# Weight chunks of four blocks instead of two, and the residual in DRAM during the FFNs, in a decoder layer

## The chip, the cores and the metric

The kernel runs on one core of one Trainium2 chip. The metric is the device time of one execution in microseconds (us). Five engines with instruction streams of their own work side by side and wait for each other by semaphores: TensorE (PE: matmuls, with the weight loads listed apart as PEld), VectorE (DVE), ScalarE (ACT), GpSimd (POOL) and SyncE (SP), which issues most of the DMAs.

## The reference

One decoder layer on 256 tokens of width 2048, in float32: a SwiGLU FFN of width 5504 as a half step, a mixer of two gated linear attentions, and a second SwiGLU half step. Each sub-layer has an RMSNorm before it and one after it, ahead of the residual add.

```python
def swiglu(x, w_gate, w_up, w_down):
    return (jax.nn.silu(x @ w_gate) * (x @ w_up)) @ w_down

    f1 = swiglu(rms_norm(h, ffn1_pre_norm[l]), ffn1_w_gate[l], ffn1_w_up[l], ffn1_w_down[l])
    h = h + 0.5 * rms_norm(f1, ffn1_post_norm[l])
    m = hybrid_token_mixer(rms_norm(h, mix_pre_norm[l]), l, w_in[l], ...)
    h = h + rms_norm(m, mix_post_norm[l])
    f2 = swiglu(rms_norm(h, ffn2_pre_norm[l]), ffn2_w_gate[l], ffn2_w_up[l], ffn2_w_down[l])
    h = h + 0.5 * rms_norm(f2, ffn2_post_norm[l])
```

The mixer projects its input with w_in into eleven pieces (queries, keys, values, gates), runs two chunked linear attentions, weights both with sigmoid gates, adds them and projects with w_out. Nearly all of the work is in the products with the weight matrices, which are read from HBM once.

## The kernel before

**A product.** Each float32 operand is split into a rounded part (hi, made by ACT) and a rest (lo, made by DVE: value minus hi), both in the fast float32r format. One product of a 128x128 piece of the activations with a 128x512 block of weights is three matmuls, hi*hi, lo*hi, hi*lo (`mm3`, lines 157 to 159). The 256 tokens are two tiles, t = 0 and 1. PE's results collect in PSUM tiles.

**Weights.** `wload` and `wchunk` (lines 129 to 148) bring a chunk of two 128x512 blocks by one DMA of SP into a raw buffer; `split_into` (line 150) makes hi (ACT, line 151) and lo (DVE, line 153), each in one instruction of 1024 columns. The pool `ring` has five buffers each of raw, hi and lo, 1024 columns wide (RING = 5, RW = 1024). A raw buffer is free again when DVE has made lo from it, a hi and a lo buffer when PE has used them.

**Units and sevens.** `gemm_pair` (line 329) computes two output blocks i = 0, 1 for both token tiles. Its depth of 2048 is 8 units of two weight rows of blocks, so a unit has four weight blocks and eight products. Some units are computed as a "seven", with seven products instead of eight, from sums and differences of weight blocks (`Blocks.seven`, line 265; the activations' sums are made once by `operand_sums`). A seven loads its four blocks with four DMAs of one block into two raw buffers, ra and rb. DVE makes three sums more (lines 279, 281, 283), into a row tile `wsum` and back into rb; ACT makes the hi parts (lines 278, 280, 282, 284); DVE the lo parts (the three adds under `issue_after` and behind it, line 243 in the profile, since `add` is a helper). Row tiles come from the pool `rows`: three buffers of 3x512 columns, all under one tag. A seven takes three of them, for wsum and for its hi and lo part (wsumh, wsuml). `Blocks.share` (line 304), which ends the sevens of a block, takes two, and `operand_sums` and `sums_of` take some too.

The lists SUMS (units 2, 4, 6) and FOUR (2, 4, 5, 6) say which units are sevens; the FFN's eleven blocks of `w_gate` and `w_up` have none in the first block of FFN 1, then FOUR and SUMS in turn. The mixer's pairs use SUMS, and FOUR where its sums are there. The list `steps` (line 346) sets the order. With SUMS the sevens stand in their natural places; with FOUR and with `late=True` (five pairs of the mixer) they stand with half a plain unit, one chunk, between them:

```python
        if late:
            at = range(6, 6 + 2 * len(sevens), 2)
        elif len(sevens) > len(SUMS):
            at = range(3, 3 + 2 * len(sevens), 2)
```

`down_proj` (line 587) goes through w_down in two halves of 1024 columns, with six sevens in each half (DSUMS and DMORE), and holds the last DTAIL = 7 rows of the second half back, split in buffers that are free by then, so that token tile 0 can be finished first. `out_proj` (line 534) does the same for w_out with TAIL = 4. Both load the next stage's first chunks ahead (`following`, AHEAD = 3 in out_proj). `gemm_block` (line 161) is the plain form; with `held` it computes tile 0 over the whole depth first and keeps the chunks for tile 1.

**Side work.** Transposes, norms and the attentions are Python generators in `Side`; `pump` advances them by a step between the products.

**The residual** h is eight SBUF tiles of 128x512 (line 110). During the mixer it lies in DRAM (`away`, line 112), and its SBUF tiles hold gates.

**The order of work.** The framework that builds the kernel lays out each engine's instructions in order of priority, that of the program where nothing stands against it, and gives tiles of one tag their buffers as these come free. On the chip each engine runs its list in order.

Of the kernel before, what the change touches and what calls it, by code (L numbers as in the profile page):

```python
# [7 lines left out]
F32 = mybir.dt.float32  # L8
# [7 lines left out]
P = 128  # L16
# [11 lines left out]
RW = 2 * CB  # L28
STEPS = ((3, 2, 2, 2), (6, 1, 1, 1))
RING = 5  # L30
AHEAD = 3
# [55 lines left out]
def kernel(ctx: ExitStack, tc: tile.TileContext, a: dict, out: bass.AP):  # L87
# [22 lines left out]
    h = [[hpool.tile([P, CB], F32, name=f"h{t}_{n}") for n in range(4)] for t in range(NT)]  # L110

    away = [[dram.tile([P, CB], F32, name=f"away{t}_{n}") for n in range(4)] for t in range(NT)]
# [10 lines left out]

    def ring_alloc(w):
        hi, lo = [ring.tile([P, RW], F32R, tag=s, name=nm(s))[:, :2 * w]
                  .rearrange("p (i c) -> p i c", i=2) for s in ("whi", "wlo")]
        return [(hi, lo)]

    def wload(src: bass.AP, w: int, apart=False):
        raw = ring.tile([P, RW], F32, tag="raw", name=nm("raw"))[:, :2 * w].rearrange(  # L130
            "p (i c) -> p i c", i=2)
        for i in range(2) if apart else [slice(0, 2)]:
            nc.sync.dma_start(raw[:, i, :], src[:, i, :])
        return raw, apart

    def wchunk(src: bass.AP, w: int, alloc=ring_alloc, raw=None):


        raw, apart = raw or wload(src, w)
        parts = alloc(w)  # L140
        if len(parts) == 1:
            hi, lo = parts[0]
            for i in range(2) if apart else [slice(0, 2)]:
                split_into(hi[:, i, :], lo[:, i, :], raw[:, i, :])
            return [(hi[:, i, :], lo[:, i, :]) for i in range(2)]
        for i, (hi, lo) in enumerate(parts):
            split_into(hi, lo, raw[:, i, :])
        return parts
# [12 lines left out]
    def gemm_block(w_dram, c0, w, lhs, nkt=KT, held=None, raws=(), ready=()):  # L161
# [4 lines left out]
        raws, ready = list(raws), list(ready)  # L166
        nb = -(-w // CB)
        step = 2 // nb
        pss = [[ps_tile(f"mm{t}") for _ in range(nb)] for t in range(NT)]

        def chunk(k0, alloc):
            if ready:
                return ready.pop(0)
            raw = raws.pop(0) if raws else None
            src = w_dram[k0 * P:(k0 + step) * P, c0:c0 + w]
            return wchunk(src.rearrange("(k p) c -> p k c", p=P) if nb == 1 else
                          src.rearrange("p (n c) -> p n c", n=nb), w // nb, alloc, raw)

        def mm(t, k0, parts):
            for i, part in enumerate(parts):  # L180
                kt = k0 + i % step
                mm3(pss[t][i // step][:, :w // nb], lhs(t, kt), part, kt == 0, kt == nkt - 1)

        if held is None:
            for k0 in range(0, nkt, step):
# [3 lines left out]
                side.pump()  # L189
        else:  # L190
            kept = []
            for i, k0 in enumerate(range(0, nkt, 2)):
                kept.append((k0, chunk(k0, ring_alloc if i < RING else held)))
                mm(0, *kept[-1])
                side.pump()
            for k in kept:
                mm(1, *k)
                side.pump()
# [46 lines left out]
    class Blocks:  # L245
# [19 lines left out]
        def seven(self, u, end):  # L265
            w, k0 = self.w, 2 * u
            ra, rb = [ring.tile([P, RW], F32, tag="raw", name=nm("raw"))[:, :2 * w]
                      .rearrange("p (i c) -> p i c", i=2) for _ in range(2)]
            wsum, hi, lo = [row_tile(n, d)[:, :, :w] for n, d in
                            (("wsum", F32), ("wsumh", F32R), ("wsuml", F32R))]  # L270

            nc.sync.dma_start(ra[:, 0, :], self.block(0, k0))
            nc.sync.dma_start(ra[:, 1, :], self.block(1, k0 + 1))
            nc.sync.dma_start(rb[:, 0, :], self.block(1, k0))
            nc.sync.dma_start(rb[:, 1, :], self.block(0, k0 + 1))

            (ahi, alo), (bhi, blo) = ring_alloc(w) + ring_alloc(w)
# [1082 lines left out]
```

## Time and profile before

| | |
|---|---|
| median of 3 runs | 2084.71 us (2083.17 to 2084.87) |
| profiled execution, first to last instruction | 2083.3 us |
| PE, PEld busy | 2069.5 us (99%), 1722.0 us (83%) |
| DVE, ACT busy | 1855.3 us (89%), 1240.8 us (60%) |
| moved by DMA | 412.24 MB, 198 GB/s in the mean |
| granted TensorE clock, mean | 0.998 |

The profiled execution's time is known as its span. In lists of groups a row has the line, the engine, the operation, out<-in by the program's names, the count, then busy time and mean duration in ns, then the idle time before and what ended it. In a timeline a row has the start and the duration in us, then engine, line and operation; brackets give idle time before it. In a list of waits a row has who waited for whom, the us in total, the times and the longest. FFN 1 runs to about 680 us, the mixer to about 1394, FFN 2 to the end.

### The profile page before, as it was taken

Reading aid. Unit: us, or ns where it says so; the run is one execution under the profiler, and the core shown is the slowest. Engines: PE = TensorE matmul, PEld = TensorE weight load, DVE = VectorE, ACT = ScalarE, POOL = GpSimd, SP = SyncE. Lnnn points to the kernel's source line nnn. Section 1 sums busy time; section 2 is a strip of 40 time slices with the busy share of each in tenths; the row PEclk is TensorE's granted clock in tenths of the full one; section 3 lists DMA queues with packets and bytes.
Section 4 is the critical chain, followed back from the end, with each engine's and each line's share of the span. In section 5 each row is a group of like instructions: output and inputs, shape, how many; then the busy total and the mean of one; then the engine's idle time right before and its main releaser. Section 6 shows DMA issues by size and latency. Waiting matters only on the chain.

```text
span 2083.3 us, 29324 instructions
## 1 busy us (share of the span) xinstructions
PE 2069.5 (99%) x10509; PEld 1722.0 (83%) x10509; DVE 1855.3 (89%) x2187; ACT 1240.8 (60%) x1670; POOL 40.7 (2%) x87
## 2 busy tenths in 40 slices
PE   9999999999999999999999999999999999999998
PEld 7888888898888888878888888888888888898886
DVE  7898999989899779989999897578999989999896
ACT  6555656566666575576655554465555655666663
POOL 1000000000000100000000000010000000000000
PEclk9999999999999999999999999999999999999999
DMA  8666656667767466555566566755665656576663
GB/s 267 184 209 201 213 187 197 210 185 223 216 191 235 148 201 210 159 172 188 178 195 195 178 220 216 221 182 171 222 197 188 207 187 225 164 238 202 202 206 128
DMA packets 200666, 412.24 MB, mean 198 GB/s; under 512 B 18036, under 2 KB 26423, under 8 KB 200520
## 3 DMA queue, kind: packets, MB, share of 16 engines
q1 hardware_dynamic: 194896, 401.80, 60.9%
q10 hardware_dynamic: 5624, 8.57, 1.4%
q8 instruction: 82, 1.34, 0.3%
q14 instruction: 64, 0.52, 0.1%
HBM read 406.11 MB, written 4.19 MB: 197 GB/s over the span
## 4 chain that ended last, share of the span: by engine, by line
PE 96%; ACT 2%; DVE 1%; issue 1%; DMA 0%; POOL 0%; SPq 0%; DVEq 0%; POOLq 0%; ACTq 0%
PE c L157 22%; PE c L159 21%; PE c L158 21%; PE p L159 5%; PE p L157 5%; PE p L158 5%; PE mm L157 3%; PE mm L159 3%; PE mm L158 3%; PE ps L397 2%; PE acc L157 1%; PE acc L158 1%; PE acc L159 1%; PE ps L905 0%; DVE h L510 0%
## 5 line engine op out<-in xcount | busy, mean ns | idle before, releaser
L151 ACT ACTIVATE whi<-raw 128x1024 fp32r<-128x1024 f32 (+3 forms) x498 | 511.0, 1033 | 284.8 <-PE c L158 116.8
L153 DVE TENSOR_TENSOR wlo<-raw,whi 128x1024 fp32r<-128x1024 f32 (+3 forms) x498 | 587.7, 1190 | 85.5 <-ACT whi L151 84.2
L157 PE MATMUL c<-whi,xhi 128*128 128x512 f32 (+1 forms) x1270 | 495.8, 391 | 0.1
L159 PE MATMUL c<-wlo,xhi 128*128 128x512 f32 (+1 forms) x1270 | 490.9, 387 | 0.0
L158 PE MATMUL c<-whi,xlo 128*128 128x512 f32 (+1 forms) x1270 | 490.6, 386 | 0.0
L243 DVE TENSOR_TENSOR wlo<-raw,whi 128x1024 fp32r<-128x1024 f32 (+1 forms) x252 | 294.5, 1202 | 12.2 <-ACT whi L278 6.1
L159 PEld LDWEIGHTS c<-wlo,xhi 128*128 128x128 f32 x1270 | 238.5, 188 | 47.5 <-DVE wlo L153 0.3
L157 PEld LDWEIGHTS c<-whi,xhi 128*128 128x128 f32 x1270 | 238.6, 188 | 46.3 <-ACT xhi L469 0.5
L158 PEld LDWEIGHTS c<-whi,xlo 128*128 128x128 f32 x1270 | 238.7, 188 | 45.0
L282 ACT ACTIVATE whi<-raw 128x1024 fp32r<-128x1024 f32 (+1 forms) x126 | 131.8, 1046 | 203.9 <-DVE raw L243 80.9
L243 DVE TENSOR_TENSOR wsuml<-wsum,wsumh 128x1536 fp32r<-128x1536 f32 (+1 forms) x126 | 218.1, 1731 | 36.8 <-ACT wsumh L284 36.5
L157 PE MATMUL c<-whi,hkhi 128*128 128x512 f32 x558 | 217.0, 389 | 0.0
L159 PE MATMUL c<-wlo,hkhi 128*128 128x512 f32 x558 | 216.8, 388 | 0.0
L158 PE MATMUL c<-whi,hklo 128*128 128x512 f32 x558 | 216.7, 388 | 0.0
L280 ACT ACTIVATE wsumh<-wsum 128x1024 fp32r<-128x1024 f32 (+1 forms) x126 | 131.6, 1045 | 107.4 <-DVE wsum L243 70.5
L278 ACT ACTIVATE whi<-raw 128x1024 fp32r<-128x1024 f32 (+1 forms) x126 | 131.6, 1044 | 103.0 <-PE c L158 87.7
L243 DVE TENSOR_TENSOR wsum<-raw,raw 128x1024 f32<-128x1024 f32 (+1 forms) x126 | 151.8, 1205 | 21.6 <-DMA raw<-in_ffn_w_down_dram 18.1
L159 PEld LDWEIGHTS c<-wlo,hkhi 128*128 128x128 f32 x558 | 104.7, 188 | 21.6
L158 PEld LDWEIGHTS c<-whi,hklo 128*128 128x128 f32 x558 | 104.7, 188 | 21.4
L157 PEld LDWEIGHTS c<-whi,hkhi 128*128 128x128 f32 x558 | 104.7, 188 | 21.1
L243 DVE TENSOR_TENSOR c<-c,psum 128x512 f32<-128x512 f32 (+1 forms) x135 | 86.5, 683 | 11.8 <-PE c L159 11.4
L243 DVE TENSOR_TENSOR wsum<-raw 128x512 f32<-128x512 f32 (+1 forms) x126 | 86.0, 683 | 3.5
(347 smaller groups left out, 3119.4 us busy)
## 6 DMA issues: line engine op xcount, KB each, us to landing
raw<-in_ffn_w_down_dram SPq DMA_DIRECT2D x124, 512.0 KB, 4.5
raw<-in_w_in_dram SPq DMA_DIRECT2D x104, 512.0 KB, 4.5
raw<-in_ffn_w_up_dram SPq DMA_DIRECT2D x97, 512.0 KB, 4.6
raw<-in_ffn_w_gate_dram SPq DMA_DIRECT2D x96, 512.0 KB, 4.7
raw<-in_ffn_w_gate_dram SPq DMA_DIRECT2D x128, 256.0 KB, 3.7
raw<-in_w_in_dram SPq DMA_DIRECT2D x128, 256.0 KB, 3.5
raw<-in_ffn_w_up_dram SPq DMA_DIRECT2D x126, 256.0 KB, 3.8
raw<-in_ffn_w_down_dram SPq DMA_DIRECT2D x96, 256.0 KB, 4.2
```

What stands on the lines that cost most here:

```text
L151: last[0] = nc.scalar.activation(hi, src, AF.Copy)
L153: nc.vector.tensor_tensor(lo, src, hi.bitcast(F32), op=ALU.subtract)
L157: nc.tensor.matmul(ps, lhsT=xhi, rhs=whi, start=start, stop=False)
L158: nc.tensor.matmul(ps, lhsT=xlo, rhs=whi, start=False, stop=False)
L159: nc.tensor.matmul(ps, lhsT=xhi, rhs=wlo, start=False, stop=stop)
L243: return nc.vector.tensor_tensor(o, x, y, op=op)
L278: nc.scalar.activation(ahi, ra, AF.Copy)
L280: nc.scalar.activation(hi[:, 0:2, :], wsum[:, 0:2, :], AF.Copy)
L282: nc.scalar.activation(bhi, rb, AF.Copy)
L397: end = nc.tensor.transpose(dst_ps[:, i * P:(i + 1) * P], src[:, i * P:(i + 1) * P], ident)
```

## The change

A chunk becomes four blocks, so that one ACT and one DVE instruction make hi and lo of 2048 columns.

- RW is 2048, RING 3 (hi and lo), and raw buffers are counted apart: RAWS = 2. `raw_tile` takes a raw buffer; while `roomy` is set, two of four turns take a buffer of the tag "hold" instead, the place of the residual.
- The residual is one tile per token tile, under the tag "hold". FFN 2 stores it to DRAM (`away2`) after its first block of w_gate; FFN 1 doesn't store it, since it is the input x. `residual()` in the second half of `down_proj`, after unit 6, clears `roomy` and loads it back. `roomy` is set after the first block of each FFN.
- A plain unit of `gemm_pair` is one chunk: two DMAs of two blocks each into one raw buffer, one split. In `gemm_block` a chunk is four rows of weights, in `out_proj` one row by 2048 columns, in `down_proj` two rows by 1024.
- A seven takes one raw buffer and three row tiles. Two of its four blocks are loaded into the row tile `own`. Four columns of blocks, two loaded and two sums, stand in raw; two loaded blocks and one sum stand in own. The products from raw come first, the three from own last.
- The order of sevens in steps of whole units: FOUR at (1, 3, 5, 6), late at (3, 4, 5), SUMS at their own places.
- AHEAD is 2, the `hn` tiles are gone (the product is formed in the silu tile), and the tail of `down_proj` is taken in chunks of one, two and four rows. The last FFN piece of 384 columns moves to the activations' place.

The matmuls are the same ones. Core of the diff:

```diff
-RW = 2 * CB
+RW = 4 * CB
-RING = 5
-AHEAD = 3
+RING = 3
+RAWS = 2
+AHEAD = 2
...
+    def raw_tile(w):
+        turn[0] += 1
+        if roomy[0] and turn[0] % (RAWS + NT) >= RAWS:
+            raw = hpool.tile([P, RW], F32, tag="hold", name=nm("raw"), bufs=NT)
+        else:
+            raw = ring.tile([P, RW], F32, tag="raw", name=nm("raw"), bufs=RAWS)
+        return raw[:, :4 * w].rearrange("p (i c) -> p i c", i=4)
...
         def seven(self, u, end):
-            ra, rb = [ring.tile([P, RW], F32, tag="raw", name=nm("raw"))[:, :2 * w]
-                      .rearrange("p (i c) -> p i c", i=2) for _ in range(2)]
-            wsum, hi, lo = [row_tile(n, d)[:, :, :w] for n, d in
-                            (("wsum", F32), ("wsumh", F32R), ("wsuml", F32R))]
...
+            raw = raw_tile(w)
+            own, ohi, olo = [row_tile(n, d)[:, :, :w] for n, d in
+                             (("wsum", F32), ("wsumh", F32R), ("wsuml", F32R))]
+            load(raw, 1, self.block(0, k0))
+            load(raw, 0, self.block(1, k0))
+            load(own, 0, self.block(1, k0 + 1))
+            load(own, 1, self.block(0, k0 + 1))
+            hi, lo = ring_alloc(w)[0]
+            add(raw[:, 2, :], raw[:, 1, :], raw[:, 0, :])
+            nc.scalar.activation(hi[:, 1:3, :], raw[:, 1:3, :], AF.Copy)
+            add(raw[:, 0:4:3, :], raw[:, 0:3:2, :], own[:, 0:1, :].broadcast_to([P, 2, w]))
+            nc.scalar.activation(hi[:, 0:4:3, :], raw[:, 0:4:3, :], AF.Copy)
+            summed = add(own[:, 2, :], raw[:, 3, :], own[:, 1, :])
+            last[0] = nc.scalar.activation(ohi, own, AF.Copy)
             with tc.issue_after(summed.ins):
+                add(lo, raw, hi.bitcast(F32), ALU.subtract)
+            add(olo, own, ohi.bitcast(F32), ALU.subtract)
+            shared, single = [[(x[:, i, :], y[:, i, :]) for i in range(n)]
+                              for x, y, n in ((hi, lo, 4), (ohi, olo, 3))]
...
+            self.product("p1", self.lhs(0, k0), shared[1], end)
+            self.product("p6", self.part("s2", u), shared[3], end)
+            self.product("p5", self.part("d", u), shared[2], end)
+            self.product("p7", self.part("s3", u), shared[0], end)
             side.pump()
+            self.product((0, 1), self.part("s4", u), single[0])
+            self.product((0, 0), self.lhs(0, k0 + 1), single[1])
+            self.product((1, 0), self.lhs(1, k0 + 1), single[2])
             side.pump()
...
+    def load_unit(ws, u, w):
+        raw = raw_tile(w)
+        for i, (w_dram, c0) in enumerate(ws):
+            load(raw, slice(2 * i, 2 * i + 2), rows_of(w_dram, 2 * u, 2, c0, w))
+        return raw
...
-        steps = [(u, i) for u in range(nu) if u not in sevens for i in range(2)]
+        steps = [u for u in range(nu) if u not in sevens]
         if late:
-            at = range(6, 6 + 2 * len(sevens), 2)
+            at = range(3, 3 + len(sevens))
         elif len(sevens) > len(SUMS):
-            at = range(3, 3 + 2 * len(sevens), 2)
+            at = (1, 3, 5, 6)
         else:
-            at = [2 * u - j for j, u in enumerate(sevens)]
+            at = sevens
...
+            def residual():
+                roomy[0] = False
+                new_h()
+                for t in range(NT):
+                    nc.sync.dma_start(hrow[t], a["x"][t * P:(t + 1) * P, :].rearrange(
+                        "p (n c) -> p n c", c=CB) if begin else away2[t])
...
             return down_proj(a[pre + "_w_down"], FKT, lhs, sums_of, post, pre_next,
-                             [held_x] + [ring_alloc] * 2 + [held] * 4, then)
+                             [(1, held_x), (2, ring_alloc), (4, held)], residual, then)
```

More of the change, by code (lines that the diff above doesn't have):

```diff
@@ L624, in down_proj @@
             units = sorted(DSUMS + DMORE[hf])
-            kt = 0
-            while kt < n:
-                u = kt // 2
-                if kt % 2 == 0 and u + 1 in units and u + 1 not in parts:
+            for kt in range(0, n, 2):
+                u, m = kt // 2, min(2, n - kt)
+                if u + 1 in units and u + 1 not in parts:
                     parts[u + 1] = sums_of(u + 1)
@@ L691, in held @@
             def held(w):
[L692 to L694 removed]
+                return [[fpool.tile([P, 2, w], F32R, tag="hT", name=nm("held"), bufs=FKT // 4)
+                         for _ in range(2)] for _ in range(2)]
             xl = lhs_of(x)
```

337 lines of the change are left out of this document (175 added, 162 removed).

## The prediction

> **What bounds the kernel now.** I read the page's totals first, then PE's own waits, then the chain that ended last.
>
> ```profile
> span 2083.3 us, 29324 instructions
> PE 2069.5 (99%) x10509; PEld 1722.0 (83%) x10509; DVE 1855.3 (89%) x2187; ACT 1240.8 (60%) x1670; POOL 40.7 (2%) x87
> PE 96%; ACT 2%; DVE 1%; issue 1%; DMA 0%; POOL 0%; SPq 0%; DVEq 0%; POOLq 0%; ACTq 0%
> ```
> ```profile
> PE p L157 <- ACT hqT L839: 2.5, 1, 2.5
> PE ps L1300 <- POOL idle L1295: 1.3, 1, 1.3
> ```
>
> The reader is to see that TensorE (PE) carries 96% of the chain, and that in 2083 us it waited for another engine hardly ever: the one wait of note is 2.5 us. A modelled end can hide small gaps, so the pitch of the matmuls is read next: three of them, one product (hi*hi, lo*hi, hi*lo), start 0.68 us before the next three (302.91 to 303.59). A plain unit of four weight blocks is eight products, 5.44 us; a seven is seven products, 4.76 us. So PE bounds the kernel, and its work is the same in both kernels: the lists of sevens and the products in each are unchanged.
>
> ```profile
> 302.91 0.39 PE L157 MATMUL c<-whi,xhi 128*128 128x512 f32 x1
> 303.59 0.39 PE L157 MATMUL c<-whi,xhi 128*128 128x512 f32 x1
> ```
>
> That leaves two questions: which waits of PE can go, and which can come. VectorE (DVE) is the engine that could make them. Stage by stage (columns: PE, PEld, DVE, ACT, POOL busy with counts, clock, DMA share, GB/s; two blocks of FFN 1, then one of the mixer):
>
> ```profile
> 264.00:306.00 42.00, 42.00 (x191) 34.85 (x190) 40.27 (x40) 24.36 (x29) 0.00 (x0) 1.00 0.58 186
> 306.00:348.00 42.00, 42.00 (x192) 34.84 (x190) 38.24 (x40) 24.25 (x28) 0.00 (x0) 1.00 0.68 214
> 968.00:1010.00 42.00, 42.00 (x434) 34.03 (x433) 41.46 (x70) 29.02 (x48) 0.99 (x2) 1.00 0.53 165
> ```
>
> DVE is busy 40.27 and 38.24 of 42 us in the FFN, 41.46 in the mixer, and PE is never idle beside it. DVE is nearly the second bound; PE is still the first.
>
> **The merged instructions.** Their prices, by form:
>
> ```profile
> L153 DVE TENSOR_TENSOR wlo<-raw,whi 128x1024 fp32r<-128x1024 f32 x462 | 558.4, 1218 | 75.3 <-ACT whi L151 74.0
> L151 ACT ACTIVATE whi<-raw 128x1024 fp32r<-128x1024 f32 x462 | 484.9, 1056 | 267.2 <-PE c L158 110.3 <-issue 36.6 <-PE mm L158 34.5
> L243 DVE TENSOR_TENSOR wsuml<-wsum,wsumh 128x1536 fp32r<-128x1536 f32 x119 | 208.6, 1753 | 36.4 <-ACT wsumh L284 36.1
> L243 DVE TENSOR_TENSOR wsum<-raw 128x512 f32<-128x512 f32 x119 | 82.1, 690 | 3.3
> L284 ACT ACTIVATE wsumh<-wsum 128x512 fp32r<-128x512 f32 x119 | 73.5, 618 | 8.0 <-DVE wsum L243 8.0
> ```
>
> DVE takes 0.69, 1.22 and 1.75 us for 512, 1024 and 1536 columns, 0.53 a step; 2048 is then 2.28 us (estimate). ACT takes 0.62 and 1.06 us; 1536 is 1.49 and 2048 1.93 us (estimates). Merging 462 splits into 231 saves DVE 231 x (2 x 1.218 - 2.28) = 36 us. In a seven DVE had 512+512+1024+1024+1024+1536, that is 6.8 us, and gets 512+512+1024+2048+1536, 6.6 us: 119 times, 19 us more. ACT saves 231 x 0.18 + 119 x 0.19 = 64 us. All of it lies beside PE: the path gains nothing, except perhaps at the single 2.5 us wait for ACT. After that wait the matmuls start 0.43 us apart instead of 0.23 for about nine of them:
>
> ```profile
> 763.01 0.39 PE L157 MATMUL c<-whi,xhi 128*128 128x512 f32 x1
> 765.86 0.50 PE L157 MATMUL p<-whi,xs 128*128 128x512 f32 x1 [2.46 <-ACT hqT L839]
> 766.70 0.63 PE L157 MATMUL p<-wsumh,xs 128*128 128x512 f32 x1
> 767.13 0.63 PE L158 MATMUL p<-wsumh,xs 128*128 128x512 f32 x1
> ```
>
> So the wait costs 2.6 us and the slow stretch 8 x 0.2 = 1.6 us: 4.2 us is all that the middle of the kernel can give back. I take 0, since the wait is for a transpose copy (L839), not for a split.
>
> **The new load into a seven's own tile.** Here lies the price. Before, a seven loads its four blocks into two of five raw buffers, and DVE writes the sums into a row tile. After, two blocks land by DMA directly in a row tile (own). Row tiles have three buffers under one tag, and a seven takes all three: own, and the rounded and rest halves of it, ohi and olo. In the next seven, own's load can start only when olo of this one has been made, for olo is the last reader of own; and ohi waits until PE is done with this seven's last products, as the row halves already do:
>
> ```profile
> ACT wsumh L280 <- PE c L158: 36.2, 39, 7.4
> ```
>
> A load costs, over the five "late" blocks of the mixer,
>
> ```profile
> DMA to landing us min/median/max: 2.6/3.8/5.3
> ```
>
> I take 2.6, as SP has been blocked and the queue is empty. Now the late blocks: their order was plain halves between the sevens, and becomes seven, seven, seven. Count from T, where PE ends the first: ohi of the second 1.49, olo 1.75, own of the third lands 2.6 later, DVE adds (1024) 1.22, ACT rounds 1.06, DVE's rest (2048) 2.28: T + 10.4. PE meanwhile has the second seven and two matmuls of the third, 4.76 + 0.45 = 5.2 us. PE stands for 5.2 us, whatever lead DVE had: 5 blocks, 26 us.
>
> The second seven can be late as well. Its own load starts when the first's olo ends, and its rest is ready 2.6 + 1.22 + 1.06 + 2.28 = 7.2 us after that, where PE wants it 2.04 us (three products) after wanting olo. A lead under 5.1 us is then a wait. The leads before, in a late block and in a FOUR block of the FFN:
>
> ```profile
> 907.96 1.75 DVE L243 TENSOR_TENSOR wsuml<-wsum,wsumh 128x1536 fp32r<-128x1536 f32 x1
> 909.76 0.50 PE L159 MATMUL p<-wsuml,xs 128*128 128x512 f32 x1
> ```
> ```profile
> 289.12 1.76 DVE L243 TENSOR_TENSOR wsuml<-wsum,wsumh 128x1536 fp32r<-128x1536 f32 x1 [0.50 <-ACT wsumh L284]
> 292.48 0.39 PE L159 MATMUL p<-wsuml,hkhi 128*128 128x512 f32 x1
> ```
>
> DVE ends at 909.71 and PE takes it at 909.76: no lead. In the FFN it ends at 290.88 and is taken at 292.48: 1.6 us. With no lead the late block pays 5.1 us for the second and, since olo then follows its rest by 1.75 where PE has 2.72, 5.1 - 1.0 = 4.1 for the third: 9.2 in all, against 5.2 with full lead. I take 2 us a block over the floor: 10 us. For the clock, half of the 1.6 us seen above, five times: 4 us. The Trainium skill, TensorE: Matmul & The Clock Gate, Part 1, has the clock halved after an idle window of about 3.4 us and for one such window; here 2.46 us was enough. By that page five waits over 3.4 us would cost an estimated 5 x 1.7 = 8.5 us, and the sum would be 4.5 us higher.
>
> FOUR blocks (five in each FFN, two in the mixer by the code's alternation) get one pair of adjacent sevens each. The wait is 5.1 less the lead: 0 if DVE is 5 us ahead, which the order of ohi and olo just allows, 3.5 us with the 1.6 us of today. I take the middle, 1.7: 12 times, 20 us. SUMS blocks keep plain units between the sevens (10.2 us a pair against a chain of 2.6 + 1.22 + 1.06 + 2.28 + 1.75 = 8.9): nothing.
>
> Against all of these: PE's order is fixed when the kernel is built, and may be fixed so that the two products of the next plain unit that no seven touches go first, 1.36 us each of 17 times, 23 us. The records show the order as written; between 0 and 23 I take 12 off.
>
> **The smaller edits.** Raw buffers fall from five of two blocks to two of four, and four while the residual is out. The landings:
>
> ```profile
> raw<-in_w_in_dram SPq DMA_DIRECT2D x104, 512.0 KB, 4.5
> raw<-in_w_in_dram SPq DMA_DIRECT2D x128, 256.0 KB, 3.5
> ```
>
> By these 1 MB lands in about 6.5 us (estimate); with the split, 1.93 + 2.28, one slot turns in 10.7, two give a unit each 5.4 us, against PE's 5.44 in plain stretches. That is just enough in the mixer; the bounds are 0 and 0.5 us a unit (below). In FFN 1's first block PE has to start on two units instead of two and a half: 0 to 4, I take 2. At the end of each down projection seven weight rows pass the two slots while PE wants them within two units: 0 to 4 each, I take 4 for both. The residual is a matter of bytes and of SP's queue:
>
> ```profile
> DMA packets 200666, 412.24 MB, mean 198 GB/s; under 512 B 18036, under 2 KB 26423, under 8 KB 200520
> ```
>
> It adds 6 MB to 412 (one reload in FFN 1, a store and a reload in FFN 2) at a DMA share of 0.53 to 0.68; its reload sits in SP's queue between weight loads, and waits there until both of its buffers are split: 0 to 6.5 each, I take 3 for both. Below nothing none of these can go, for PE shows no wait there now. The pumps move, but their number per block stays.
>
> Sum: 26 + 10 + 4 + 20 - 12 + 2 + 4 + 3 = 57 us. The profiled execution spans 2083.3, the median of the runs is 2084.7, 1.4 more (launch edges and run to run). 2083.3 + 57 + 1.4 = 2142 us.
>
> **The rivals.** (1) PE hides it: the order leaves every seven a lead of over 5 us, and lighter ACT work removes the wait at 763 us. It decides if PE shows no wait for a rest at all. Gain up to 4.2: 2080.5. For it: DVE has 55 us less to do. Against: in the late block DVE had no lead at all. (2) It is hidden, and nothing else moves: 2084.7. (3) Only the coarser pieces count: a product waits for a rest of 2.28 where 1.22 was enough, so leads under 1.06 us turn into waits, three sevens in the late block shown, 3.2 us, 2088. The Trainium skill, Perfetto Trace Analysis, Optimizing Scalar/DVE Operations, says that where Scalar/Vector aren't saturated but make bubbles elsewhere, instructions should be broken up; a DVE at 89% is near that case. (4) Two raw slots bind the mixer: its ten blocks of two weights, eight units each, lose 0.5 us a unit to queueing behind attention on DVE (41.46 of 42 us), 40 us, without any wait for own: 2125. For: 5.4 against 5.44. Against: PE may run three chunks behind the splits.
>
> **How the numbers follow.** Forecast 0.62, (1) 0.12, (2) 0.07, (3) 0.07, (4) 0.12. A difference under 0.2%, 4 us, is about what measuring can't tell from none. Faster 0.12; same 0.07 + 0.07 = 0.14; slower 0.62 + 0.12 = 0.74. The low end takes in (2) and (3) and ends at (1): 2080. At the high end late blocks cost 9.2 + 1.6 each (54), FOUR blocks 2.5 (30), the small edits 18: 102, 2187. The forecast's own range is 2104 (the floor of 26 less 5 x 1.36, and nothing else) to 2187.
>
> **What would show it.** PE waits for "wlo" or for the own tile's rest in the third seven of each late block, about 5 us, with clock digits below 9 from 840 to 1100 us; SP's queue waiting for the DVE line that makes olo; rests of 2048 columns near 2.28 us; DVE's busy time down by about 55. The forecast is wrong if PE's busy share stays at 99% and PE's waits hold no such line, or if they name DMA into raw instead.

## The result, and the profile after

The changed kernel takes 2297.8 us (median of 4 runs, 2296.6 to 2303.3) against 2084.8: ratio 1.103, 95% interval 1.102 to 1.104, 213 us slower. The forecast was 2142: the direction is right, but the loss is nearly four times the 57 us of the sum, and the time lies far above the range of 2104 to 2187.

The page's totals of the changed kernel, and the shares of its chain:

```profile
span 2295.1 us, 27656 instructions
...
PE 2154.4 (94%) x10509; PEld 1743.9 (76%) x10509; DVE 1830.9 (80%) x1812; ACT 1196.4 (52%) x1295; POOL 51.0 (2%) x87
...
PE 6%; DVE 3%; DMA 2%; issue 1%; ACT 1%; POOL 0%; SPq 0%; DVEq 0%; POOLq 0%; ACTq 0%
```

The span grew by 211.8 us. PE's idle time grew by 126.9 of these (140.7 against 13.8), and its busy time by 84.9 for the same 10509 matmuls: they start further apart. No other engine filled up: DVE fell from 89% to 80% busy. The chain's shares add up to 13%, so it was lost on the way and can't be read here. PE's waits can (in total, times, longest):

```profile
PE p L170 <- ACT whi L296: 60.7, 28, 4.4
PE c L170 <- ACT whi L164: 20.9, 10, 4.2
PE p L172 <- DVE wlo L259: 14.3, 27, 1.5
```

L296 rounds a seven's second pair of weights, which DVE makes with a block that lands in the own tile. That wait is new. DVE's, and what SP's queue waited for:

```profile
DVE raw L259 <- DMA wsum<-in_ffn_w_up_dram: 92.0, 44, 4.6
DVE raw L259 <- DMA wsum<-in_w_in_dram: 40.6, 14, 5.5
DVE raw L259 <- DMA wsum<-in_ffn_w_down_dram: 16.7, 9, 3.4
```
```profile
SPq L150 <- DVE wlo L259: 755.0, 111, 13.6
...
SPq L150 <- DVE wsuml L259: 64.6, 76, 3.6
```

So DVE waits 149 us for the own tile's load. SP's first row is the wait for a free raw tile (e10 comes back to it); in the second, 76 times, the own tile's load waits for the last reader of the seven before (wsuml, olo in the code). One FOUR block of FFN 1 shows how. SP's issues, then DVE, then PE (start, duration, what; in brackets the idle time before):

```profile
314.31 0.37 SPq L150 DMA_DIRECT2D raw<-in_ffn_w_gate_dram  x1
314.73 0.47 SPq L150 DMA_DIRECT2D raw<-in_ffn_w_up_dram  x1
315.98 0.34 SPq L150 DMA_DIRECT2D wsum<-in_ffn_w_up_dram  x1
```
```profile
314.20 1.75 DVE L259 TENSOR_TENSOR wsuml<-wsum,wsumh 128x1536 fp32r<-128x1536 f32 x1
320.27 1.23 DVE L259 TENSOR_TENSOR raw<-raw,wsum 128x1024 f32<-128x1024 f32 x1 [4.32 <-DMA wsum<-in_ffn_w_up_dram]
...
322.62 2.29 DVE L259 TENSOR_TENSOR wlo<-raw,whi 128x2048 fp32r<-128x2048 f32 x1 [0.40 <-ACT whi L296]
324.83 1.75 DVE L259 TENSOR_TENSOR wsuml<-wsum,wsumh 128x1536 fp32r<-128x1536 f32 x1
```
```profile
318.18 0.39 PE L171 MATMUL c<-whi,xlo 128*128 128x512 f32 x1
322.64 0.80 PE L170 MATMUL p<-whi,hkhi 128*128 128x512 f32 x1 [4.07 <-ACT whi L296]
...
323.66 0.63 PE L170 MATMUL p<-whi,hkhi 128*128 128x512 f32 x1
324.09 0.63 PE L171 MATMUL p<-whi,hklo 128*128 128x512 f32 x1
```

DVE ends olo at 315.95, SP issues the next own load 0.03 us later, behind the 1 MB of the next plain unit that it issued 1.2 to 1.7 us before; DVE has the load at 320.27. From the end of one olo to the end of the next (324.83 + 1.75 = 326.58) one turn takes **10.63 us**. PE needs 4.76 us between two adjacent sevens and 10.2 where a plain unit lies between them. So DVE gains no lead in the block, and at the adjacent pair PE stands for 4.07 us and then starts a matmul each 0.43 us instead of 0.23. What the whole block looks like, with the next one (columns as in the prediction's windows):

```profile
282.00:334.00 52.00, 46.93 (x196) 36.94 (x195) 41.59 (x35) 26.18 (x23) 0.00 (x0) 0.93 0.52 177
334.00:376.00 42.00, 40.46 (x181) 32.68 (x180) 34.38 (x27) 19.96 (x17) 0.00 (x0) 1.00 0.55 181
```

The first row holds the FOUR block shown: 52 us for 196 matmuls, where 42 us held 191 in the kernel before.

Where it all went is seen from the sevens, 126 in each kernel, counted in order of time. The mark of a seven is the start of the weight load of its last matmul (c<-wsuml). The table takes the marks of each kernel, less those of the kernel before, and gives what each stretch adds; e1, e12 and e16 are experiments below. The last column is what the new order of sevens and plain units would do to the marks by itself, with PE always busy; it is the same for the four kernels, and has to be taken off each of them.

| stretch (sevens) | changed | e1 | e12 | e16 | order alone |
|---|---|---|---|---|---|
| up to the first (0) | 1.4 | 2.9 | 1.6 | 0.3 | 0 |
| FFN 1, pairs of up and gate (0 to 34) | 48.8 | 1.2 | 0.8 | 0.5 | 0 |
| FFN 1, down (34 to 46) | 10.2 | 4.3 | 2.7 | 0.1 | 0 |
| into the mixer (46 to 52) | 8.0 | 8.3 | 13.9 | -0.7 | 0 |
| mixer, late blocks (52 to 67) | 41.0 | 13.7 | 9.9 | 4.2 | -5.4 |
| behind them (67 to 68) | 14.6 | 15.1 | 11.7 | 2.7 | 2.7 |
| rest of the mixer's pairs (68 to 78) | 9.7 | 1.4 | -0.8 | 3.1 | 2.7 |
| mixer to FFN 2 (78 to 79) | 17.8 | 17.9 | 20.1 | -1.9 | -2.7 |
| FFN 2, pairs (79 to 110) | 48.1 | 4.0 | 3.1 | 2.9 | 2.7 |
| FFN 2, end and down (110 to 125) | 10.5 | 2.7 | 2.4 | 0.2 | 0 |
| sum | 210.1 | 71.5 | 65.4 | 11.4 | 0 |

The last column comes from the code: half a plain unit is 2.72 us of products, the third seven of a late block now stands two halves earlier, and the first of a FOUR block one half. It is the work, not the waits, that lies elsewhere; in e12, where PE is full in the FOUR blocks, mark 17 comes 2.7 us earlier against the kernel before than marks 16 and 18 do. So the late blocks of the changed kernel cost 46 us and not 41, the gap behind them 12 and not 15, and the pairs of FFN 2 45. (In e2 and e6 the late sevens stand so that mark 67 isn't shifted: there only the 2.7 of mark 68 counts.)

### The profile page after: what moved, and what is told of

Its sections match the earlier page's. It is cut to its first block, busy times and chain, and to the rows that moved or that the text cites. A ratio compares the mean times of both kernels' runs of the same rounds, so it can differ in the third digit from the quotient of the medians.

```text
span 2295.1 us, 27656 instructions
## 1 busy us (share of the span) xinstructions
PE 2154.4 (94%) x10509; PEld 1743.9 (76%) x10509; DVE 1830.9 (80%) x1812; ACT 1196.4 (52%) x1295; POOL 51.0 (2%) x87
## 5 line engine op out<-in xcount | busy, mean ns | idle before, releaser
L164 ACT ACTIVATE whi<-raw 128x2048 fp32r<-128x2048 f32 (+4 forms) x254 | 468.2, 1847 | 344.9 <-DMA raw<-in_w_in_dram 107.2
L166 DVE TENSOR_TENSOR wlo<-raw,whi 128x2048 fp32r<-128x2048 f32 (+4 forms) x254 | 558.4, 2201 | 108.6 <-ACT whi L164 108.2
L172 PE MATMUL c<-wlo,xhi 128*128 128x512 f32 (+1 forms) x1168 | 433.8, 388 | 4.9 <-DVE wlo L166 4.9
L259 DVE TENSOR_TENSOR wlo<-raw,whi 128x2048 fp32r<-128x2048 f32 (+1 forms) x126 | 284.9, 2261 | 84.9 <-ACT whi L296 84.1
L259 DVE TENSOR_TENSOR raw<-raw,wsum 128x1024 f32<-128x1024 f32 (+1 forms) x126 | 152.1, 1207 | 149.9 <-DMA wsum<-in_ffn_w_up_dram 92.0
L296 ACT ACTIVATE whi<-raw 128x1024 fp32r<-128x1024 f32 (+1 forms) x126 | 131.9, 1047 | 191.9 <-DVE raw L259 187.2
L298 ACT ACTIVATE wsumh<-wsum 128x1536 fp32r<-128x1536 f32 (+1 forms) x126 | 183.9, 1459 | 12.6 <-DVE wsum L259 8.2
L172 PE MATMUL c<-wlo,hkhi 128*128 128x512 f32 x456 | 177.8, 393 | 0.3 <-DVE wlo L166 0.3
L170 PE MATMUL p<-whi,hkhi 128*128 128x512 f32 (+1 forms) x258 | 104.6, 405 | 43.0 <-ACT whi L296 42.9
L259 DVE TENSOR_TENSOR raw<-raw 128x512 f32<-128x512 f32 (+1 forms) x126 | 83.8, 676 | 23.8 <-DMA raw<-in_ffn_w_up_dram 11.1
L171 PE MATMUL p<-whi,hklo 128*128 128x512 f32 (+1 forms) x258 | 101.2, 397 | 0.0
```

Of the source, the lines that this page charges most:

```text
L164: last[0] = nc.scalar.activation(hi, src, AF.Copy)
L166: nc.vector.tensor_tensor(lo, src, hi.bitcast(F32), op=ALU.subtract)
L170: nc.tensor.matmul(ps, lhsT=xhi, rhs=whi, start=start, stop=False)
L171: nc.tensor.matmul(ps, lhsT=xlo, rhs=whi, start=False, stop=False)
L172: nc.tensor.matmul(ps, lhsT=xhi, rhs=wlo, start=False, stop=stop)
L259: return nc.vector.tensor_tensor(o, x, y, op=op)
```

## The experiments

Theory A: the own tile's load stands in a serial chain (last reader, load, add, rounding, rest), since three row tiles are all there is; that chain is most of the loss. Its rivals: B, the coarse pieces of 2048 columns; R, the two raw tiles; C, side work (attention steps fed in between products) that is held back for longer. In every kernel here all of the computation is done. Each time is the median of 4 runs, beside 2083.6 to 2085.1 for the kernel before.

**e1: all four blocks in the raw tile.** The sums move to the row tile, and no DMA goes there; the seven products follow in the order of the kernel before again.

```
-            load(own, 0, self.block(1, k0 + 1))
-            load(own, 1, self.block(0, k0 + 1))
+            load(raw, 1, self.block(1, k0 + 1))
+            load(raw, 3, self.block(0, k0 + 1))
...
-            add(raw[:, 0:4:3, :], raw[:, 0:3:2, :], own[:, 0:1, :].broadcast_to([P, 2, w]))
+            add(own[:, 0:2, :], raw[:, 0:2, :], raw[:, 2:3, :].broadcast_to([P, 2, w]))
```

> The changed kernel, but a seven loads all four of its blocks into the raw buffer, and DVE makes the three sums of the row tile; instruction counts and sizes of a seven stay (DVE 512, 512, 1024, 1536, 2048; ACT 1024, 1024, 1536), and so do chunks, buffers and order. Theory A (the load into the row tile, which can't start before the previous seven's last rest, is the cost): some 140 of the 213 us go, about 2155; what stays is the adjacent sevens of the late blocks (T + 8.5 against 5.2 us, five times, with the slow clock behind it 25) and the stalls around the attentions. Theory B (coarser pieces and fewer raw buffers are the cost): within 20 us of 2298, as both stay.

2157.4 us (2154.5 to 2160.8): 140 of the 213 us are gone, with the sizes of the pieces, the tiles and the counts of instructions unchanged. The wait for L296 nearly went with them:

```profile
PE c L170 <- ACT whi L296: 9.0, 7, 1.7
PE c L170 <- ACT whi L164: 6.9, 5, 2.2
```

So B, whose pieces are still there, isn't what those 140 us are. The FFN pairs cost about 1 us each now, less the order; some 70 us are left elsewhere.

**e2: late sevens spread.**

```
-            at = range(3, 3 + len(sevens))
+            at = sevens
```

> The changed kernel with the late blocks' sevens at their natural places, a plain unit between any two. Theory A: the five late blocks lose the 41 us that they gained and keep about 8: 2265. Theory B: no change, 2298; if keeping the attention's steps ahead of the sevens matters more, slower than 2298, since these blocks leave less room ahead of the first seven.

2277.2 (2273.9 to 2278.5), 21 faster, short of the 33 that A asks. Less the order, the late stretch fell from 46 to 18 us, and the gap behind it (67 to 68) rose from 12 to 20.

**e3: the own load on the queue of POOL.**

```
-            load(own, 0, self.block(1, k0 + 1))
-            load(own, 1, self.block(0, k0 + 1))
+            nc.gpsimd.dma_start(own[:, 0, :], self.block(1, k0 + 1))
+            nc.gpsimd.dma_start(own[:, 1, :], self.block(0, k0 + 1))
```

> The changed kernel with the two loads into the row tile issued by GpSimd instead of SyncE, so that they don't stand behind a plain unit's loads in SyncE's list. Theory A with landing time as the size: they land in about 3 us instead of 4.3, 1.3 us less at some 30 places where PE waits, 2298 - 40 = 2258. If the wait for the buffer is the whole of it, and not the queue: within 15 us of 2298. Theory B: no change.

2306.1 (2304.0 to 2307.3), 8 slower. The landings of the own tile, in the changed kernel and in e3:

```profile
DMA to landing us min/median/max: 2.6/4.2/6.8
```
```profile
DMA to landing us min/median/max: 2.9/3.8/7.4
```

The median falls by 0.4 us, where theory A by landing time asked for 1.3, and nothing is gained. A queue of its own doesn't help; that the moment at which the load may start is what counts is shown by e12.

**e4: side work held back later.** The changed kernel sets side.full, which stops heavy side steps for the rest of a block, at the start of the plain unit ahead of a seven; before, that was half a unit ahead. The edit sets it in the second half of that unit.

```
-            if any(v in sevens for v in steps[j:j + 2]):
-                side.full = True
             if u in sevens:
+                side.full = True
...
+                if i and any(v in sevens for v in steps[j + 1:j + 2]):
+                    side.full = True
                 side.pump()
```

> The changed kernel, but heavy side work (the attentions) is held back only from the second half of the plain unit ahead of the first seven, as the kernel before did, not from its start: one step more per block. Theory C (the attentions are pushed past the blocks that hid them, and PE waits for them at the ends): 25 to 35 us of the 213 go, about 2268. Theories A and B: within 10 us of 2298.

2281.8 (2278.5 to 2285.8): 16 faster, the gap at 67 to 68 down from 14.6 to 1.9. C is real, at about half the size I gave it.

**e5: e1 and e4 together.**

> The changed kernel with two edits together: a seven's four blocks all land in the raw tile (as in e1, 2157.4 alone), and heavy side work is held back only from the second half of the plain unit ahead (as in e4, 16 us gained alone). Theory A (the serial chain through the own tile is the cause of some 140 of the 213 us, and the held-back side work a separate cause of some 15): 2157 - 15 = 2142, within 6, and the gap between sevens 67 and 68 falls from +15 to about +2. Rival (the gain of e4 was only cover for waits that e1 takes away as well): 2157, within 4.

2146.7 (2144.2 to 2147.4): 11 less than e1, and inside the 2136 to 2148 of separate causes. The gap at 67 to 68 fell to 2.4 as forecast, but the late stretch rose from 13.7 to 24.0, so part of the gain is lost again there; I take it that attention that runs earlier is what costs it.

**e6: e5 with the late sevens spread.**

> The same with the late blocks' sevens at their natural places (2, 4, 6) as a third edit. In e1 the late stretch still cost 13.7 us (sevens 52 to 67). Theory A (adjacent sevens wait there for the coarse split, so spreading them takes that away): 2142 - 12 = 2130, within 7. Rival (spread sevens hold back attention, which then comes later): 2142 or more. Either way the kernel before, 2084.8, is not reached, since the tails of the down projections and the steps between stages (46 to 47, 78 to 79) keep their two raw tiles.

2152.7 (2149.5 to 2156.9), 6 slower than e5. The rival holds: less the order, the late stretch itself fell from 29 to 10 us, and the gap behind it rose from 0 to 20. Up to seven 68 both had lost 39.5. Where adjacent sevens no longer wait for a load, spreading them gains nothing; that it moves attention is how I read it.

**e7: the own load alone, in the kernel before.**

```
-            nc.sync.dma_start(rb[:, 0, :], self.block(1, k0))
-            nc.sync.dma_start(rb[:, 1, :], self.block(0, k0 + 1))
+            nc.sync.dma_start(own[:, 0, :], self.block(1, k0 + 1))
+            nc.sync.dma_start(own[:, 1, :], self.block(0, k0 + 1))
```

(Order of adds and products as in the changed kernel; two-block chunks, five raw tiles and the residual stay.)

> One part of the change alone, made to the kernel before: a seven's blocks (1, k+1) and (0, k+1) land in the row tile instead of a raw tile, the sums and the order of the products as in the changed kernel; chunks of two blocks, five raw tiles, and the residual stay as before. Theory A (the chain last reader of own, load, add, rounding, rest, is the price): one turn of the chain is landing 2.6 to 4.2, add 1.22, rounding 1.06, rest 1.22, row rest 1.75 and row rounding 1.49, 9.1 to 10.4 in all, against a pitch of 7.5 us where half a plain unit lies between two sevens, so 1.6 to 2.9 us for each of 36 such pairs in the FOUR blocks and 10 in the late ones: 74 to 134 us slower, 2159 to 2219. Rival (it is the coarse pieces of 2048 columns and the two raw tiles that cost, not the tile that the load lands in): within 15 us of 2085.

2149.8 (2144.3 to 2150.5): 65 slower, 9 below the range of A and far from the rival's 15. DVE's waits there:

```profile
DVE raw L243 <- DMA wsum<-in_ffn_w_up_dram: 58.1, 35, 3.3
DVE raw L243 <- DMA wsum<-in_w_in_dram: 27.4, 16, 6.0
DVE raw L243 <- DMA wsum<-in_ffn_w_down_dram: 16.5, 10, 3.9
```

The load into a row tile, with the order of adds and products that goes with it, does harm with fine pieces and five raw tiles too. In the changed kernel, where sevens stand closer together, taking it away is worth 140 (e1).

**e8: no FOUR blocks.**

```
-FOUR = (2, 4, 5, 6)
+FOUR = (2, 4, 6)
```

> The changed kernel with three sevens (units 2, 4, 6) in every block that had four (2, 4, 5, 6), so that no two sevens are adjacent outside the late blocks: one product more in each of 12 blocks, 12 x 0.68 = 8 us of TensorE more. Theory A (the adjacent sevens at the end of a FOUR block, and the pairs with one plain unit between them at little lead, pay about 100 us in both FFNs together, almost all at the adjacent pair): 2298 - 100 + 8 = 2206, within 20. Rival (the price is spread over all sevens or lies in the plain units): 2280 to 2306.

2190.2 (2189.4 to 2193.6): 107.6 less, in spite of 8 us more of products. The FOUR blocks cost about 116 us more than blocks of three sevens would in their place.

**e9: splits in halves (on e5).**

```
-            split_into(hi[:, :m, :], lo[:, :m, :], raw[:, at:at + m, :])
+            for i in range(0, m, 2):
+                j = min(i + 2, m)
+                split_into(hi[:, i:j, :], lo[:, i:j, :], raw[:, at + i:at + j, :])
```

> e5 (2146.7) with every rounding and rest of a weight chunk outside the sevens made in two instructions of 1024 columns instead of one of 2048. DVE gets some 127 x (2 x 1.218 - 2.20) = 30 us more of work, ACT 127 x (2 x 1.056 - 1.85) = 33 us. Theory D (of the 62 us that are left, most come from coarse pieces: in e5 DVE waits 22 us of 310 in the late stretch for roundings of 1.0 and 1.85 us): 10 to 25 us faster, 2122 to 2137. Theory R (they come from having two raw tiles, whatever the size of the instructions): 2143 to 2155.

2138.0 (2130.6 to 2139.9): 9 faster, just short of the range. Coarse splits outside the sevens cost some 9 us; those inside them weren't divided.

**e10: three raw tiles (on e5).**

```
-RING = 3
-RAWS = 2
+RING = 2
+RAWS = 3
```

> e5 (2146.7) with three raw tiles of four blocks instead of two, paid for with one pair less of the rounded and rest tiles (two instead of three). Theory R (loads come late, since two raw tiles are all there is in the mixer, and SP waits for a rest there before each load): 15 to 40 us faster, 2107 to 2132, if two pairs are enough for TensorE, as a unit's split (1.85 + 2.20 = 4.05) is shorter than its 5.44 of products. Theory D: within 4 us of 2147, or slower, since a split then waits for the unit before last to be multiplied.

2114.9 (2114.4 to 2116.4): 32 faster, with a pair of rounded and rest tiles less. R is real. The same stretch of late blocks, 701 to 708 matmuls, in the kernel before, in e5 and in e10:

```profile
918.00:1014.00 96.00, 96.00 (x708) 78.24 (x707) 93.91 (x136) 61.69 (x95) 3.40 (x6) 1.00 0.59 183
```
```profile
938.00:1042.00 104.00, 99.42 (x701) 77.04 (x699) 91.93 (x118) 59.68 (x79) 3.91 (x5) 0.98 0.51 165
```
```profile
924.00:1024.00 100.00, 97.54 (x703) 76.83 (x702) 92.88 (x118) 60.47 (x80) 3.02 (x5) 1.00 0.53 171
```

DVE had 2 idle us of 96 before, 12 of 104 in e5, 7 of 100 in e10. It is nearly the bound here, and with few raw tiles it has less loaded to work ahead on.

**e11: four raw tiles of two blocks in the kernel before, instead of five** (bufs=4 on the raw tile, nothing else).

> The kernel before (2084.6) with four raw tiles of two blocks instead of five: as many bytes as the two tiles of four blocks that the change leaves in the mixer, in the old small pieces. Theory R (the bytes held raw are what counts): 15 or more slower, 2100 to 2130. Theory D (the pieces count): below 2092.

2098.9 (2098.0 to 2100.3), 15 slower: at the edge of what R asks, and well above the rival's 2092.

**e12: a fourth row tile, own load kept.** The edit that takes the wait away from the changed kernel itself:

```
-RING = 3
+RING = 2
...
-    rows = ctx.enter_context(tc.tile_pool(name="rows", bufs=3))
+    rows = ctx.enter_context(tc.tile_pool(name="rows", bufs=4))
```

> The changed kernel, with the two blocks still landing in the own tile, but with four row tiles instead of three, paid for with one pair less of the rounded and rest tiles (two instead of three). The next seven's own load then has a tile that was free a whole seven earlier. Theory A (the wait for the tile, not the load, is the price): about 115 to 140 us faster, 2158 to 2183. Rival (the landing of 4.2 us in the path, or DVE's order, is the price): at most 30 faster, 2268 or more.

2152.9 (2152.0 to 2156.1): **145 us faster**, a little more than A said, though two blocks still land in the own tile, and with a pair of rounded and rest tiles less. PE's wait for L296, 60.7 us in the changed kernel, is nearly gone. PE's wait, then SP's and DVE's rows at an adjacent pair of e12:

```profile
PE p L170 <- ACT whi L296: 1.9, 3, 0.9
```

```profile
288.72 0.41 SPq L150 DMA_DIRECT2D wsum<-in_ffn_w_up_dram  x1
289.18 0.43 SPq L150 DMA_DIRECT2D wsum<-in_ffn_w_gate_dram  x1
```
```profile
292.18 1.75 DVE L259 TENSOR_TENSOR wsuml<-wsum,wsumh 128x1536 fp32r<-128x1536 f32 x1
293.85 1.22 DVE L259 TENSOR_TENSOR raw<-raw,wsum 128x1024 f32<-128x1024 f32 x1
...
298.44 1.76 DVE L259 TENSOR_TENSOR wsuml<-wsum,wsumh 128x1536 fp32r<-128x1536 f32 x1
```

The load of the next seven is issued 3.5 us before olo starts instead of behind its end, DVE goes from olo to the next add without a break, and a turn takes 6.27 us (293.93 to 300.20) instead of 10.63. PE is then full in the FOUR block:

```profile
266.00:308.00 42.00, 42.00 (x191) 34.87 (x190) 40.30 (x34) 24.47 (x21) 0.00 (x0) 1.00 0.65 218
308.00:350.00 42.00, 42.00 (x191) 34.88 (x190) 36.36 (x30) 22.82 (x19) 0.00 (x0) 1.00 0.54 183
```

The Trainium skill, Perfetto Trace Analysis, Optimization Strategy, says that a bubble which repeats along a stretch, on the engine that should be saturated, can mean that there isn't enough SBUF for the next tile. The trace agrees: one tile more takes PE from 46.93 of 52 us to 42.00 of 42.

**e13: e12 with three raw tiles and the later hold of e4.**

> e12 with three raw tiles and with heavy side work held back from the second half of the plain unit ahead, that is e10 (2114.9) with the own load kept and a fourth row tile. Theory A: as e10, 2108 to 2125, though two blocks of every seven still land in the own tile. Rival: 2150 or more.

2123.7 (2121.7 to 2125.5), as A has it. Against e10 the own load costs 9 us once it has its tile.

**e14: e10 with four raw tiles and halves; e15: e10 with four row tiles and halves.**

> e10 (2114.9) with four raw tiles and with the splits outside the sevens in halves of 1024 columns (as e9, 8.7 us gained alone). If the last 30 us are raw tiles and piece size: 2093 to 2104. If they are something else (attention that the coarser order pushes to the end of the mixer): 2107 to 2115.

> e10 (2114.9), four blocks in raw tiles, with a fourth row tile and with the splits in halves. If a lack of row tiles for the three sums holds back the sevens of the late blocks (10 us there in e10): 2096 to 2103. If not: e10 less what halves bring, 2104 to 2110.

2108.0 (2107.0 to 2108.8) and 2106.2 (2104.9 to 2107.3). They are 7 and 9 faster than e10, about what halves gave in e9: neither a fourth raw tile nor a fourth row tile brings more than a microsecond or two once the own load is gone.

**e16: e15 with heavy side work held back only from the first seven in FOUR blocks.**

```
-                if i and any(v in sevens for v in steps[j + 1:j + 2]):
+                if i and len(sevens) <= len(SUMS) and any(v in sevens for v in steps[j + 1:j + 2]):
```

> e15 (2106.2) with heavy side work in FOUR blocks held back only from the first seven itself: as many heavy steps ahead of it as in the kernel before (two of the pumps there; e15 leaves one). If the held-back steps are what lies between sevens 78 and 79: 2096 to 2102. If they are few enough to be made up elsewhere: 2104 to 2108.

2097.8 (2096.3 to 2099.5), 8 faster. The same 50 us at the mixer's end, in e15 and in e16:

```profile
1253.00:1303.00 50.00, 45.30 (x213) 37.48 (x212) 32.35 (x45) 20.73 (x40) 2.41 (x4) 0.93 0.49 162
```
```profile
1253.00:1303.00 50.00, 50.00 (x239) 41.70 (x237) 41.53 (x49) 24.18 (x30) 0.00 (x0) 1.00 0.66 220
```

In e15 PE still waits here for steps of attention, at 45.30 of 50 us and a clock of 0.93; in e16 they are done, and PE is full.

**e17: e15 with the residual kept in SBUF.** The store in FFN 2, both reloads and roomy[0] = True are taken out, so that the FFNs have three raw tiles instead of five.

> e15 (2106.2) with the residual kept in SBUF through both FFNs, as before the change: its store in FFN 2 and both reloads are left out, and its place holds no raw weights, so that the FFNs too have three raw tiles in place of five. The prediction took 3 us for the residual. If its bytes or its place in SP's queue cost that: 2101 to 2104. If the two tiles that its place gives are needed in the FFNs: 2110 or more. If neither: 2105 to 2107.

2107.2 (2104.9 to 2108.5): no difference that can be told from e15. The edit takes out two things at once, so the time alone would also allow that they cancel. The marks speak against it: the FFN pairs, where the two raw tiles serve, add 0.5 and 2.9 us in e15 and in e17 alike, and the down projections, where the residual is loaded back, are no faster without it (0.3 and 0.1 in e15, 1.3 and 1.7 in e17). So beside three raw tiles neither counts; beside the changed kernel's two this wasn't tried.

No version is faster than the kernel before. The best, e16, is still 0.6% slower (1.006, 1.005 to 1.008). Less the order, 9.6 of its 11.4 us lie in the late blocks, and there between adjacent sevens: from one mark to the next it is 4.8 to 7.0 us, where PE's work is 4.76. DVE's turn for a seven without a wait for a load was 6.27 us in e12, and the kernel before had half a plain unit between such sevens, 7.48 us from mark to mark. So what is left looks like DVE's own work on a seven, set closer than DVE can do it; an experiment on e16 for this is missing, and so is one with a fourth row tile beside three pairs of rounded and rest tiles.

## Why the prediction was right in direction and wrong in size

**What bounds the kernel.** Right: PE bound it, its work stayed the same, and the price came as waits.

**FOUR blocks, 20 us forecast: the step that failed.** The sum took "the middle, 1.7" of a wait of 5.1 us less a lead. The chain was the right one; its landing, its lead and its clock were not. The landing was taken as 2.6 us, the least of the row shown there (median 3.8), "as SP has been blocked and the queue is empty". In the block shown it was 4.29, with the plain unit's 1 MB issued shortly ahead; this alone brings the turn from 8.9 to 10.6 us. The lead was read from the trace of before, 1.6 us; but a turn over 10.2 builds no lead between sevens that are a plain unit apart, so none is left for the adjacent pair. And PE then runs on at 0.43 us a matmul. The marks of this pair are these two rows:

```profile
316.59 0.19 PEld L172 LDWEIGHTS c<-wsuml,xhi 128*128 128x128 f32 x1
328.81 0.19 PEld L172 LDWEIGHTS c<-wsuml,xhi 128*128 128x128 f32 x1
```

They lie 12.22 us apart, 7.5 more than PE's 4.76: 4.07 of wait, and about 3.4 of clock (last section). By the table's marks, less the order, the FOUR blocks cost some 92 us (FFN 1 42.5, FFN 2 41.9, mixer 7.3), 7.6 each where 1.7 was forecast; taken out, in e8, they gave back 116. The range had the same fault: its high end took 2.5 a block, although the price without a lead was already worked out as 5.1.

**SUMS blocks, 0 forecast.** Measured 10 us in both FFNs between the FOUR blocks, about 1.2 a block, by the same chain: 10.2 a pair was set against 8.9, and a turn took 10.6.

**Late blocks, 40 with their clock.** Measured 46, less the order. The wait is where it was forecast: from the second to the third seven of the five blocks the marks lie 9.5 to 12.4 us apart, 33 us more than the work, against 26 and the clock. But part of the agreement is luck: e12, which hardly waits for the own tile, still loses 15 us there, and this share was not in the sum.

**Clock, 4 us.** Far too low, because there were many more waits. The granted clock was 0.974 over the whole span, against 0.998: 0.026 x 2295 - 0.002 x 2083 = 56 us of it not granted. The page of the Trainium skill that I weighed (TensorE: Matmul & The Clock Gate, Part 1) gave an estimate of 8.5 for five waits. The count of waits was wrong, whichever price is used.

**PE's order, -12.** Not seen in the block shown: ahead of the wait there are two matmuls of the next plain unit (the last at 318.18), 0.45 us, where 1.36 was allowed. The plain unit's rest stood behind the seven in DVE's order, while DVE was idle for 4.32 us.

**Raw tiles, "just enough in the mixer", 0 us; rival (4), 40 us.** e10 gives 32 us for one more raw tile, over the whole kernel. The rival was right in kind and near in size. The mistake was to set it beside the forecast as another outcome; the two causes add.

**"The pumps move, but their number per block stays."** Wrong in what counts: as many pumps, but fewer that may run a heavy step, since side.full is looked up a whole unit ahead. e4 gives 16 us for it, and e5 and e16 show 11 and 8 in parts. That is where the losses at 67 to 68 and 78 to 79 come from, 12 and 20 us less the order, which no term of the sum had: e16, with the steps back, has 0 and 1 there.

**The merged instructions.** Their durations were right (DVE 2.28, ACT 1.93 as estimates):

```profile
L166 DVE TENSOR_TENSOR wlo<-raw,whi 128x2048 fp32r<-128x2048 f32 x230 | 525.2, 2286 | 96.2 <-ACT whi L164 95.8
```
```profile
L164 ACT ACTIVATE whi<-raw 128x2048 fp32r<-128x2048 f32 x230 | 439.7, 1915 | 320.3 <-DMA raw<-in_w_in_dram 95.3 <-PE p L171 41.4 <-PE c L171 39.0
```

But DVE's busy time fell by 24 us, not 55. Neighbours overlap in the records: the rest before the olo shown above,

```profile
312.00 2.29 DVE L259 TENSOR_TENSOR wlo<-raw,whi 128x2048 fp32r<-128x2048 f32 x1 [0.40 <-ACT whi L296]
```

ends at 314.29, and olo starts at 314.20. If each of the 375 instructions saved (2187 to 1812) had 0.09 us of this, an estimate from this one pair, 34 us of the 55 had never been there. The Trainium skill, Perfetto Trace Analysis, Optimizing Scalar/DVE Operations, says that part of an instruction's profiled time overlaps with the next one; these rows agree.

**The smaller edits.** First block 2, measured 1.4. Residual 3, nothing seen in e17. Tails of the down projections 4 for both: behind the last seven PE's products took 0.9 us longer than before in FFN 1 and 1.9 in FFN 2, so that was about right. The 10.2 and 10.5 of the table lie ahead of the tails (3 of the 10.5 in FFN 2's last SUMS block), at sevens for which the sum had nothing; with the fourth row tile it is 2.7 and 2.4, so most of it was the own tile again.

**Rivals (1) to (3), and the signs.** (1) and (2) are out: PE did wait for the own tile. (3), coarse pieces only, exists as the 9 us of e9, on top. Of the signs, the waits of PE and of SP's queue came as named. The clock digits stayed at 9 in all slices, which are too long (57 us each) to show a single wait.

## What to carry to other kernels

Before a DMA is pointed at a tile from a small pool, write out one whole turn (last reader, issue, everything ahead of it in the queue, landing, first use, last reader) and set it against the shortest distance between two users in the new order: if the turn is longer than the mean distance, no lead is left for the short ones, whatever the old trace shows. Where SBUF is traded, ask of each pool which engine's work ahead it holds: here a row tile more, at the price of a pair of rounded and rest tiles, was worth 145 us, and a raw tile more at the same price 32. Causes that sit in different resources can add up; set them against each other as rivals only where one excludes the other. And a flag that looks one step ahead changes its meaning when the step gets bigger.

## What the runs showed of the hardware

A wait of PE can cost nearly twice its length here, because the clock is low behind it. The 14 us around the one shown (columns as before):

```profile
316.00:330.00 14.00, 9.93 (x32) 7.32 (x32) 9.30 (x7) 5.76 (x5) 0.00 (x0) 0.76 0.42 149
```

One wait of 4.07 us leaves a granted clock of 0.76 over 14 us, that is 3.4 us not granted. Over the kernel, PE's busy time grew by 85 us for the same matmuls, beside 127 us of waiting; the granted clock accounts for 56 of the 85, and where the rest lies is open.

The 256 KB loads into the own tile took 2.6 to 6.8 us to land. In the trace of the changed kernel the median was 3.3 us where SP had issued nothing in the 2.5 us before, and 4.6 where it had issued about 1 MB; on a queue of their own (e3) it was 3.8, against 4.2 for all of them here.
